# A fused two-model block on one core: the first stage put in written order, its state space products on VectorE alone with their matmuls by column groups, and its small loads on other queues

## The chip, the core and the metric

The kernel runs as one program on one core of a Trainium2 chip. The time is the device time of one execution in microseconds (us); the median of several runs is compared. Beside the times there is one profiled execution. In its rows PE is TensorE's matmuls, PEld its weight loads, DVE is VectorE, ACT ScalarE, POOL GpSimd; SPq and a DMA row of POOL are transfers being issued by SyncE and GpSimd.

## The reference

Two model blocks run one after the other on 256 tokens of width 1024, all in float32. The first has two attention layers (neighbourhood, then sliding window) with adaptive norms, whose shifts and scales come from a condition vector; the second has a grouped complex state space layer (S5) and a stick-breaking attention layer. What matters here is the start of the first block and the constants of the S5 layer, which the kernel works out early because they depend on weights alone:

```python
mod_lat = (silu_c @ ada_w[i] + ada_b[i])[:, None, :]      # 1024 x 6144 weights per layer
sh1, sc1, ga1, sh2, sc2, ga2 = jnp.split(mod_lat, 6, axis=-1)
u_lat = modulate(rms_norm(h_lat, g_mix[i]), sh1, sc1)     # 256 tokens; the same for 256 of context
ql, kl, vl = jnp.split((u_lat @ w).reshape(B, L, 3, H, dh), 3, axis=2)
...
a_bar = jnp.exp(lam * dt)                                 # 64 groups x 64 states, complex
b_bar = ((a_bar - 1.0) / lam)[..., None] * b_mat          # 64 x 64 x 16
bu = jnp.einsum('tbgh,gph->tbgp', u_t, b_bar)
a_cum, s = lax.associative_scan(binop, (a_elems, bu), axis=0)
y = jnp.einsum('tbgp,ghp->tbgh', s + a_cum * h0[None], c_mat).real
```

The kernel replaces the scan by chunks of 8 steps. For that it needs the powers of `a_bar` (0 to 8) times `b_bar`, called `em` or e below, their products with `c_mat` (a 128 x 128 kernel of each group pair, called k), and writes both to DRAM for the later S5 stage.

## The kernel before

A tile framework traces the program and a scheduler decides the order of the instructions on each engine; semaphores are added for every dependency. Each engine then runs its list strictly in order. Products in float32 are made of three passes: each weight is split into a high part (`whi`, by ScalarE) and a rest (`wlo`, by VectorE), the activations into `xh` and `xl`, and L299 to L301 are the three matmuls.

The first stage is L878 to L957. It holds these strands, which share the engines:

- The condition and S5 loads, the constants `cst`, and the tokens `x` and `ctx`, which TensorE transposes (L921) and ScalarE copies to `h` and `hc`.
- Sixteen ada steps (L342 to L374, `ada_step`): each loads 512 KB of `ada_w` and multiplies it by the condition in four column groups of TensorE (L357). Steps 0 to 7 make the shift, 8 to 15 the scale; after the 8th and the 16th step the sum is copied (`adacc`, L361), transposed (L364) and written to `mods`. Even steps load into three `ada` buffers, odd ones into pairs of halves `stl`, so about six steps can be in flight; a further load waits for the matmul of the step that held its buffer.
- S5's constants: `S5.__init__` makes the powers `pw` and `bb` on VectorE in small operations. `e(r, engine)` multiplies them for r = 0 to 3, each in 24 operations of 128 x 256: r = 0 and 1 on VectorE, r = 2 and 3 on GpSimd (L916, L917, L934, L940). `k1(r)` (L720, L723) multiplies e with the C matrix on TensorE into 32 columns of PSUM per group q, `et(r)` (L734) transposes e, ScalarE copies the result and SyncE writes it to `edr`; `k2(r)` (L742) transposes k.
- 22 small loads (L201, L903, L905), spread among the ada steps on SyncE.
- `rstd` (L425, L436): the sum of squares of the tokens; and `normed` (L463), which needs `mods`, makes `xh` and `xl` from the tokens, in eight steps for both streams.

The first attention stage begins with the query, key and value products of the first head pair (`g` and `sc` banks, L299 to L301), then score, softmax and the rest in chains, with the next pair's products between them (L971 to L1132). Two loops that set the order in the first stage:

```python
            s5.e(0, V)
            s5.e(2, G)
...
            for i in range(8):
                ada_step()
                some(3)
...
            for r in range(4):
                s5.k1(r)
                s5.et(r)
                s5.k2(r)
```

Of the kernel before, what the change touches and what calls it, by code (L numbers as in the profile page):

```python
# [16 lines left out]
D = 1024  # L17
# [65 lines left out]
def _build(ctx, tc, I, out, dbg):  # L83
# [3 lines left out]
    dma = nc.sync.dma_start  # L87
# [81 lines left out]
    def vector_loads(va, cc):  # L169

        def r128(ap):
            return ap.rearrange("(a b) -> a b", b=128)

        def r128l(ap):
            return ap.rearrange("l (a b) -> (l a) b", b=128)

        todo = [(cc[0:8, :], I["c"].rearrange("a (k p) -> (a k) p", p=128)),
                (cc[8:16, :], I["c_ctx"].rearrange("(k p) -> k p", p=128))]

        def rows(t, r0, src):  # L180
# [390 lines left out]
    def s5_load(pp):  # L571
# [15 lines left out]
        return (lt, ld, dr, bt, ci), [lambda o=o, i=i: dma(out=o, in_=i) for o, i in todo]  # L587

    class S5:


        def __init__(self, pp, loads):
# [55 lines left out]
            tb = [tmp_tile().rearrange("p (g h) -> p g h", h=16) for _ in range(2)]  # L648
            cmul(bb, bt, cb, tb)
# [7 lines left out]
            self.pf_, self.ph_ = pf, ph  # L657
            for r in range(2):
                act(pf[:, r], pw[r][:, 1:9, :], AF.Copy)
            u = [(cs, sn), (s_[7], s_[8])]  # L660
            for i in range(3):
                cmul((ph[:, 0], ph[:, 1]) if i == 2 else u[(i + 1) % 2], u[i % 2], u[i % 2], (t0, t1))

            self.em = [[pp.tile([128, 4, 2, 8, 16], F32, name=f"e{r}{i}") for i in range(2)] for r in range(3)]
            self.tm = [spare(2 + i, f"tm{i}").rearrange("p (i j t h) -> p i j t h", i=2, j=2, t=8) for i in range(2)]
            self.kt = [None] * 4
            self.ci, self.dr = ci, dr
# [27 lines left out]
        def save(self):  # L695
            for i in range(2):
                dma(out=cdr[:, 512 * i:512 * i + 512], in_=self.ct[i].rearrange("p g h -> p (g h)"))
            dma(out=cdr[:, 1024:1536], in_=self.pf_.rearrange("p r t g -> p (r t g)"))
            dma(out=cdr[:, 1536:1632], in_=self.ph_.rearrange("p i g -> p (i g)"))

        def e(self, r, eng):
            em, tm = self.em[r], [self.tm[eng is G][:, i] for i in range(2)]
            pa = [x_[:, 0:8, :].rearrange("p t (q j) -> p q j t", q=4)[:, :, 2 * r:2 * r + 2, :] for x_ in self.pw]
            ma = [x_.rearrange("p (q j) h -> p q j h", q=4)[:, :, 2 * r:2 * r + 2, :] for x_ in self.bb]
# [23 lines left out]
        def et(self, r):  # L728
            for q in range(4):
# [7 lines left out]
                dma(out=edr[:, 16 * q + 4 * r:16 * q + 4 * r + 4, :], in_=et)  # L737
# [128 lines left out]
    with ExitStack() as sa:  # L866
# [10 lines left out]
        pp = spp.enter_context(tc.tile_pool(name="pp", bufs=1))  # L877
        with ExitStack() as s0:  # L878
# [14 lines left out]
            for nm in ("x", "ctx"):  # L893
                for t in range(2):
                    r = [stage("h", len(xt) * 2 + j) for j in range(2)]
                    for j in range(2):
# [6 lines left out]
                lambda: dma(out=rp[:, :, 48:79],  # L903
                            in_=I["na_rpb"][0].rearrange("h r c -> (h r) c").rearrange("(p a) c -> p a c", a=2)),
                lambda: dma(out=rpad.rearrange("(p a) c -> p a c", a=2), in_=rp)]  # L905

            def some(n):
                for f in small_loads[0:n]:
                    f()
                del small_loads[0:n]  # L910

            for f in vloads[0:2] + [lambda: dma(out=cst, in_=I["cst"])] + sloads[0:5] + xloads:
                f()
            prep_cond(cc, sc)
            s5 = S5(pp, loads)
            s5.e(0, V)  # L916
            s5.e(2, G)  # L917
            for k in range(KT):
                ps = bank("x")
                for t in range(4):  # L920
                    T.transpose(ps[:, t * 128:(t + 1) * 128], xt[t][k // 4][:, (k % 4) * 128:(k % 4) * 128 + 128], ident)  # L921
                act(h[k], ps[:, 0:256], AF.Copy)
                act(hc[k], ps[:, 256:512], AF.Copy)
            for i in range(8):
                ada_step()
                some(3)
                ada_step()
                some(3)
                if i == 0:
                    for f in sloads[5:]:  # L930
                        f()
                if i == 1:
                    s5.c()
                    s5.e(3, G)  # L934
                if i == 2:
                    act(small, h[KT - 2][:, 0:1], AF.Sqrt, bias=eps, scale=0.0)
                    r = rstd(512, 0, None, "s")
                    prep_vectors(va)
                if i == 2:
                    s5.e(1, V)  # L940
            some(99)
            stt(gna, gna, 0.125, swg[:, 208:272], MUL, MUL)
            ts(gsw[0], gsw[0], 0.125, MUL)
            w = I["na_wqkv"][0]
            w_first = [Weights(wpairs(w, D, 0), by_k=True),
                       Weights(wcols(w, 2 * D, 256), by_k=True)]
            x = new_x(xa, "x", 512)
            normed(x, r, 512, lambda k, v: scg[0][:, 0, k, v:v + 1], lambda k, v: modcol(0, 0, k, v))
            for r in range(4):
                s5.k1(r)  # L950
                s5.et(r)
                s5.k2(r)
            s5.zero()
# [876 lines left out]
```

## Time and profile before

| | before |
|---|---|
| median of 3 runs | 1811.14 us (1809.02 to 1816.51) |
| the profiled execution: its time | 1810.93 us |
| its span, first to last instruction | 1809.2 us |
| busy share of the span | PE 95%, PEld 83%, DVE 66%, ACT 44%, POOL 26% |
| mean granted TensorE clock | 0.978 of full speed |

A busy share says how much of the span an engine had an instruction in work. TensorE is busy nearly throughout; its idle time is found by stretches, and the first stretch is where this change lies.

### The profile page before, as it was taken

The page shows a single profiled execution, that of the slowest core. Times are in us where ns is not written, and L with a number is a line of the kernel's source. Part 1 is how long each engine was busy: PE and PEld are TensorE (multiplying, and loading weights), DVE is VectorE, ACT ScalarE, POOL GpSimd, SP SyncE. Part 2 cuts the span into 40 slices and gives each one's busy share as a digit, 9 for nine tenths or more (in the row PEclk, how much of TensorE's full clock was granted, in tenths as well). Part 3 has the DMA queues.
Part 4 walks back from the last instruction along what each step waited for, and adds up shares of the span by engine and source line. Part 5 has one row for each costly group of instructions (what it writes and reads, how often), then busy time and mean ns, then how long its engine had stood idle before and what let it go on. Part 6 is the DMA issues. An engine that isn't in the chain of part 4 may idle for free. (4 is left out here: it accounts for less than half of the span.)

```text
span 1809.2 us, 33749 instructions
## 1 busy us (share of the span) xinstructions
PE 1717.4 (95%) x13129; PEld 1504.4 (83%) x13129; DVE 1197.0 (66%) x2508; ACT 790.6 (44%) x1446; POOL 470.6 (26%) x633
## 2 busy tenths in 40 slices
PE   5799999989999999999978999989999999999999
PEld 3478888867777777888757999978899999789998
DVE  8556877865545334447987656768577788958674
ACT  4343444433313132324655545536444465544443
POOL 5312211225789000040002000211331322424130
PEclk8899999999999999999989999999999999999999
DMA  8565555434676554332107566698458564336852
GB/s 219 174 174 160 148 169 154 109 96 134 205 220 202 180 180 141 93 97 74 53 24 186 153 196 183 208 308 225 128 154 233 150 211 142 115 97 167 231 154 88
DMA packets 441042, 286.56 MB, mean 158 GB/s; under 512 B 50450, under 2 KB 418610, under 8 KB 440882
## 3 DMA queue, kind: packets, MB, share of 16 engines
q1 hardware_dynamic: 439122, 278.64, 53.3%
q0 software_dynamic: 1760, 5.77, 0.8%
q8 instruction: 103, 1.69, 0.4%
q14 instruction: 57, 0.47, 0.1%
HBM read 271.41 MB, written 17.15 MB: 159 GB/s over the span
## 5 line engine op out<-in xcount | busy, mean ns | idle before, releaser
L108 ACT ACTIVATE whi<-raw 128x1024 fp32r<-128x1024 f32 (+2 forms) x388 | 389.7, 1012 | 487.8 <-PE g L292 353.1
L111 DVE TENSOR_TENSOR wlo<-raw,whi 128x1024 fp32r<-128x1024 f32 (+2 forms) x388 | 469.1, 1214 | 185.7 <-ACT whi L108 182.9
L293 PE MATMUL g<-xh,wlo 128*128 128x256 f32 (+1 forms) x1216 | 375.3, 309 | 5.6 <-DVE wlo L111 5.2
L291 PE MATMUL g<-xh,whi 128*128 128x256 f32 (+1 forms) x1216 | 375.5, 310 | 1.3 <-ACT xh L108 1.2
L292 PE MATMUL g<-xl,whi 128*128 128x256 f32 (+1 forms) x1216 | 374.7, 308 | 0.0
L291 PE MATMUL g<-oh,whi 128*128 128x256 f32 (+1 forms) x1056 | 332.1, 315 | 3.9 <-DVE hc L114 1.4
L293 PE MATMUL g<-oh,wlo 128*128 128x256 f32 (+1 forms) x1056 | 331.5, 314 | 0.0
L292 PE MATMUL g<-ol,whi 128*128 128x256 f32 (+1 forms) x1056 | 331.1, 314 | 0.0
L293 PEld LDWEIGHTS g<-xh,wlo 128*128 128x128 f32 x1216 | 235.4, 194 | 18.0 <-DVE wlo L111 7.4
L291 PEld LDWEIGHTS g<-xh,whi 128*128 128x128 f32 x1216 | 234.9, 193 | 16.4 <-ACT whi L108 3.5
L292 PEld LDWEIGHTS g<-xl,whi 128*128 128x128 f32 x1216 | 235.7, 194 | 9.6
L291 PEld LDWEIGHTS g<-oh,whi 128*128 128x128 f32 x1056 | 198.1, 188 | 25.1 <-issue 3.9
L292 PEld LDWEIGHTS g<-ol,whi 128*128 128x128 f32 x1056 | 198.4, 188 | 15.1 <-issue 0.9
L293 PEld LDWEIGHTS g<-oh,wlo 128*128 128x128 f32 x1056 | 198.4, 188 | 14.5 <-issue 0.3
L299 PE MATMUL g<-whi,xh 128*128 128x256 f32 x560 | 167.5, 299 | 3.8 <-ACT xh L108 2.8
L300 PE MATMUL g<-wlo,xh 128*128 128x256 f32 x560 | 161.6, 289 | 0.6 <-DVE wlo L111 0.6
L301 PE MATMUL g<-whi,xl 128*128 128x256 f32 x560 | 160.3, 288 | 0.1
L114 DVE SCALAR_TENSOR_TENSOR h<-g,mods,h 128x256 f32<-128x256 f32 x64 | 30.8, 483 | 139.1 <-PE g L293 139.1
L299 PEld LDWEIGHTS g<-whi,xh 128*128 128x128 f32 x560 | 108.3, 193 | 14.6 <-issue 10.0
L300 PEld LDWEIGHTS g<-wlo,xh 128*128 128x128 f32 x560 | 108.6, 194 | 2.0 <-DVE wlo L111 1.6
L301 PEld LDWEIGHTS g<-whi,xl 128*128 128x128 f32 x560 | 108.0, 194 | 1.1 <-issue 0.4
L108 ACT ACTIVATE oh<-t 128x256 fp32r<-128x256 f32 (+1 forms) x108 | 51.3, 482 | 125.5 <-DVE t L111 125.5
(300 smaller groups left out, 2892.0 us busy)
## 6 DMA issues: line engine op xcount, KB each, us to landing
raw<-mlp_w SPq DMA_DIRECT2D x128, 512.0 KB, 4.3
ada<-ada_w SPq DMA_DIRECT2D x88, 512.0 KB, 6.4
raw<-ffn_w_up SPq DMA_DIRECT2D x88, 512.0 KB, 5.4
raw<-ffn_w_down SPq DMA_DIRECT2D x32, 384.0 KB, 3.9
raw<-ffn_w_down SPq DMA_DIRECT2D x32, 320.0 KB
raw<-na_wqkv SPq DMA_DIRECT2D x32, 256.0 KB, 4.1
raw<-a_w_glu SPq DMA_DIRECT2D x16, 512.0 KB, 7.5
raw<-w_kv SPq DMA_DIRECT2D x16, 512.0 KB, 4.3
```

Source lines behind the costliest of these rows:

```text
L108: last[0] = A.activation(out=o, in_=i, func=f, **kw)
L111: (e or V).tensor_tensor(out=o, in0=a, in1=b, op=op)
L114: V.scalar_tensor_tensor(out=o, in0=a, scalar=s, in1=b, op0=op0, op1=op1)
L291: T.matmul(ps, lhsT=a, rhs=xh[k][:, s0:s1], start=first, stop=False)
L292: T.matmul(ps, lhsT=a, rhs=xl[k][:, s0:s1], start=False, stop=False)
L293: T.matmul(ps, lhsT=b, rhs=xh[k][:, s0:s1], start=False, stop=last_)
L299: T.matmul(ps, lhsT=xh[k][:, t0:t0 + 128], rhs=a, start=first, stop=False)
L300: T.matmul(ps, lhsT=xh[k][:, t0:t0 + 128], rhs=b, start=False, stop=False)
L301: T.matmul(ps, lhsT=xl[k][:, t0:t0 + 128], rhs=a, start=False, stop=last_)
```

## The change

Everything in the first stage up to the second weight load of the first head pair is traced inside a region in which all five engines keep the order in which the code is written. In that order the ada steps are dealt out by hand: 4, 2, 3, 2, 2 and 3 steps, with the S5 pieces between. All four `e(r)` run on VectorE, in 12 operations of 128 x 512 each, on operands that are laid out again: GpSimd copies the powers to `pw2` (eight small operations) and `bb` is written in the order that e reads. In `k1` the four column groups q are now the innermost loop. The S5 loads and the writes of `edr` and `cdr` are issued by ScalarE, the small loads by GpSimd. The pool `pp` is taken from the other end of the memory.

```diff
-    dma = nc.sync.dma_start
+    dma, dma_a = nc.sync.dma_start, nc.scalar.dma_start
...
-        return [lambda o=o, i=i: dma(out=o, in_=i) for o, i in todo]
+        return [lambda o=o, i=i, n=n: (dma if n < 2 else G.dma_start)(out=o, in_=i) for n, (o, i) in enumerate(todo)]
...
-        return (lt, ld, dr, bt, ci), [lambda o=o, i=i: dma(out=o, in_=i) for o, i in todo]
+        return (lt, ld, dr, bt, ci), [lambda o=o, i=i: dma_a(out=o, in_=i) for o, i in todo]
...
+        def tables(self):
+            pp, pw, pf, ph, u = self.pp, self.pw, self.pf_, self.ph_, self.u
+            self.pw2 = [pp.tile([128, 32, 8], F32, name=f"pz{i}") for i in range(2)]
+            for i in range(2):
+                for r in range(4):
+                    ts(self.pw2[i][:, 8 * r:8 * r + 8, :].rearrange("p (q j) t -> p q j t", q=4),
+                       pw[i][:, 0:8, :].rearrange("p t (q r j) -> p r q j t", q=4, r=4)[:, r], 1.0, MUL, 0.0, ADD, e=G)
...
-        def e(self, r, eng):
-            em, tm = self.em[r], [self.tm[eng is G][:, i] for i in range(2)]
...
-            for q in range(4):
-                cmul([x_[:, q] for x_ in em], [x_[:, q].unsqueeze(3).to_broadcast([128, 2, 8, 16]) for x_ in pa],
-                     [x_[:, q].unsqueeze(2).to_broadcast([128, 2, 8, 16]) for x_ in ma], tm, e=eng)
+        def e(self, r):
+            for hf in range(2):
+                g = slice(8 * r + 4 * hf, 8 * r + 4 * hf + 4)
+                cmul([x_.rearrange("p q j t h -> p (q j) t h")[:, 4 * hf:4 * hf + 4] for x_ in self.em[r]],
+                     [x_[:, g, :].unsqueeze(3).to_broadcast([128, 4, 8, 16]) for x_ in self.pw2],
+                     [x_[:, g, :].unsqueeze(2).to_broadcast([128, 4, 8, 16]) for x_ in self.bb], self.tm)
...
-            for q in range(4):
-                for jp in range(2):
-                    for i in range(2):
+            for jp in range(2):
+                for i in range(2):
+                    for q in range(4):
                         T.matmul(kp[32 * q:32 * q + 32, jp * 128:(jp + 1) * 128],
                                  lhsT=cbk[i][:, q, jp].rearrange("p j h -> p (j h)"),
                                  rhs=em[i][:, q, jp].rearrange("p t h -> p (t h)"), start=i == 0, stop=False)
+                for q in range(4):
                     T.matmul(kp[32 * q:32 * q + 32, jp * 128:jp * 128 + 16], lhsT=self.dd[:, 8 * q + 2 * r + jp, :],
                              rhs=C("dm")[0:32, :], start=False, stop=True)
...
-                dma(out=edr[:, 16 * q + 4 * r:16 * q + 4 * r + 4, :], in_=et)
+                dma_a(out=edr[:, 16 * q + 4 * r:16 * q + 4 * r + 4, :], in_=et)
...
-        pp = spp.enter_context(tc.tile_pool(name="pp", bufs=1))
+        pp = spp.enter_context(tc.tile_pool(name="pp", bufs=1, side="right"))
...
+            with tc.manual_schedule(engines={ENG.PE, ENG.DVE, ENG.Activation, ENG.SP, ENG.Pool}):
+                for f in vloads[0:2] + [lambda: dma(out=cst, in_=I["cst"])] + sloads + xloads + small_loads[0:15]:
+                    f()
+                prep_cond(cc, sc)
+                s5 = S5(pp, loads)
...
+                s5.tables()
+                for f in small_loads[15:]:
+                    f()
+                ada(4)
+                s5.c()
+                s5.e(0)
+                ada(2)
+                act(small, h[KT - 2][:, 0:1], AF.Sqrt, bias=eps, scale=0.0)
+                r_ = rstd(512, 0, None, "s")
+                prep_vectors(va)
+                ada(3)
+                s5.e(1)
+                operators(0)
+                ada(2)
+                w_first = [Weights(wpairs(w, D, 0), by_k=True)]
+                ada(2)
+                s5.e(2)
...
+                operators(1)
+                ada(3)
+            w_first.append(Weights(wcols(w, 2 * D, 256), by_k=True))
+            x = new_x(xa, "x", 512)
+            normed(x, r_, 512, lambda k, v: scg[0][:, 0, k, v:v + 1], lambda k, v: modcol(0, 0, k, v))
+            operators(2)
+            s5.e(3)
+            operators(3)
```

The orders below are those of the two built programs; the attention stage and what follows keep theirs but for a few hundred rows at its beginning. First VectorE, where the S5 products begin (`tm` is a partial product, `e` a result, `pw` or `pz` the powers, `bb` the B matrix, `ph` a later phase, `dd` a diagonal from the loaded `dr`). Before:

```order
L111 TENSOR_TENSOR ph<-sm 128x32
L111 TENSOR_TENSOR tm_273<-pw_198,bb_219 128x256
L111 TENSOR_TENSOR pw_199<-t 128x128
L111 TENSOR_TENSOR sm<-sm 128x32 x2
L111 TENSOR_TENSOR tm_273<-pw_199,bb_220 128x256
L111 TENSOR_TENSOR ph<-sm 128x32
L111 TENSOR_TENSOR e_267<-tm_273 128x256
```

VectorE in the same place after the change:

```order
L112 TENSOR_TENSOR pw_221<-t 128x128
L112 TENSOR_TENSOR sm<-sm 128x32 x14
L112 TENSOR_TENSOR ph<-sm 128x32
L112 TENSOR_TENSOR sm<-sm 128x32 x2
L112 TENSOR_TENSOR ph<-sm 128x32
L112 TENSOR_TENSOR dd<-dr,cst 32x1024
L112 TENSOR_TENSOR tm_361<-pz_325,bb_241 128x512
L112 TENSOR_TENSOR tm_362<-pz_326,bb_242 128x512
L112 TENSOR_TENSOR e_355<-tm_361,tm_362 128x512
```

The first e operation no longer mixes with the powers: it stands behind `dd`, and `dd` behind all of the phases. Second, TensorE at the first k1, before (`e_267` and `e_268` are the two parts of e(0), L357 is an ada step, L212 and L734 transposes):

```order
L357 MATMUL x<-ada,sl 32x256 x4
L720 MATMUL s<-e_267,cbk 32x128
L720 MATMUL s<-e_268,cbk 32x128
L734 MATMUL s<-cst,e_267 128x128 x2
L723 MATMUL s<-cst,dd 32x16
L720 MATMUL s<-e_267,cbk 32x128
L720 MATMUL s<-e_268,cbk 32x128
L212 MATMUL x<-cst,va 128x128
L723 MATMUL s<-cst,dd 32x16
```

TensorE at the first k1 after the change:

```order
L437 MATMUL s<-sd,cst 128x128 x4
L213 MATMUL x<-cst,va 128x128 x3
L358 MATMUL x<-ada,sl 32x256 x4
L358 MATMUL x<-stl_544,sl 32x256 x2
L358 MATMUL x<-stl_545,sl 32x256 x2
L365 MATMUL x<-cst,adacc 128x128 x2
L358 MATMUL x<-ada,sl 32x256 x4
L734 MATMUL s<-e_355,cbk 32x128 x4
L734 MATMUL s<-e_356,cbk 32x128 x4
L738 MATMUL s<-cst,dd 32x16 x4
```

Nine ada steps now stand before the first k1 instead of three, and four matmuls of four column groups follow each other where there were two of one group. Third, VectorE where `normed` begins, before:

```order
L111 TENSOR_TENSOR e_270<-tm_273 128x256
L114 SCALAR_TENSOR_TENSOR swg<-swg 128x64
L124 COPY adacc<-x 128x256
L111 TENSOR_TENSOR mods_71<-x,vt 128x4x2 x2
L124 COPY adacc<-x 128x256
L111 TENSOR_TENSOR mods_71<-x,vt 128x4x2 x2
L114 SCALAR_TENSOR_TENSOR scg_73<-mods_71,vt 128x16
L114 SCALAR_TENSOR_TENSOR t<-h_77,scg_73,s 128x256
```

VectorE where `normed` begins after the change:

```order
L112 TENSOR_TENSOR e_360<-tm_361,tm_362 128x512
L115 SCALAR_TENSOR_TENSOR swg<-swg 128x64
L120 TENSOR_SCALAR swg<-swg 128x64
L125 COPY adacc<-x 128x256
L112 TENSOR_TENSOR tm_361<-pz_325,bb_241 128x512
L112 TENSOR_TENSOR mods_71<-x,vt 128x4x2 x2
L112 TENSOR_TENSOR tm_362<-pz_326,bb_242 128x512
L115 SCALAR_TENSOR_TENSOR scg_73<-mods_71,vt 128x16
L112 TENSOR_TENSOR e_436<-tm_361,tm_362 128x512
L115 SCALAR_TENSOR_TENSOR t<-h_77,scg_73,s 128x256
```

The second `adacc` copy now stands behind e(0), e(1) and e(2) with the four weight splits between them, 36 operations of 128 x 512, and three of e(3)'s operations lie between it and `normed`; the other nine of e(3) stand behind `normed`.

## Rows read from the trace of the kernel before

**Rows 1.** The page: the span

```profile
span 1809.2 us, 33749 instructions
```

**Rows 2.** Windows: busy time of each engine by stretch, granted clock, DMA share

```profile
0.00:30.00 30.00, 14.62 (x102) 10.09 (x103) 21.50 (x86) 16.53 (x45) 10.08 (x21) 0.94 0.92 225
30.00:60.00 30.00, 23.77 (x183) 14.65 (x181) 28.39 (x38) 9.51 (x27) 28.04 (x38) 0.88 0.46 149
60.00:79.70 19.70, 12.48 (x105) 4.39 (x101) 5.07 (x17) 3.25 (x8) 0.41 (x1) 0.83 0.64 203
79.70:127.70 48.00, 46.74 (x366) 40.23 (x367) 26.85 (x81) 24.24 (x59) 3.88 (x6) 0.96 0.61 177
...
140.00:390.00 250.00, 247.01 (x2116) 207.38 (x2114) 193.87 (x616) 117.28 (x301) 46.70 (x55) 0.99 0.47 138
```

**Rows 3.** Timeline, 74 to 80: start, length, what, idle before

```profile
74.36 1.05 PE L357 MATMUL x<-ada,sl 128*32 128x256 f32 x8 [2.34 <-DMA ada<-ada_w]
...
77.01 0.42 DVE L124 COPY adacc<-x 128x256 f32<-128x256 f32 x1 [8.20 <-PE x L357]
...
79.68 0.79 PE L299 MATMUL g<-whi,xh 128*128 128x256 f32 x2 [1.59 <-ACT xh L108]
```

**Rows 4.** Groups on VectorE to 79.7 and on GpSimd; timeline, 20 to 22

```profile
L111 DVE TENSOR_TENSOR tm<-pw,bb 128x256 f32<-128x256 f32 x32 | 24.3, 795 | 0.5
...
L111 DVE TENSOR_TENSOR t<-bt,sm 128x512 f32<-128x512 f32 x4 | 2.7, 683 | 0.0
...
L111 POOL TENSOR_TENSOR tm<-pw,bb 128x256 f32<-128x256 f32 x32 | 24.5, 782 | 20.0 <-DVE pw L111 18.8
...
20.94 0.41 DVE L111 TENSOR_TENSOR tm<-pw,bb 128x256 f32<-128x256 f32 x1
```

**Rows 5.** TensorE: groups from 79.7 to 127.7; timeline at 89

```profile
L720 PE MATMUL s<-e,cbk 128*32 128x128 f32 x64 | 10.1, 278 | 0.3 <-ACT et L108 0.2
...
L734 PE MATMUL s<-cst,e 128*128 128x128 f32 x40 | 6.7, 306 | 0.0
...
L357 PE MATMUL x<-ada,sl 128*32 128x256 f32 x8 | 0.6, 391 | 0.0
...
89.18 0.62 PE L720 MATMUL s<-e,cbk 128*32 128x128 f32 x4
...
89.90 0.62 PE L720 MATMUL s<-e,cbk 128*32 128x128 f32 x4
```

**Rows 6.** Issues: SyncE's timeline at 4, 21 and 83; GpSimd's group

```profile
3.88 3.23 SPq L587 DMA_DIRECT2D bt<-a_b_im  x1
...
20.92 1.74 SPq L587 DMA_DIRECT2D ci<-a_c_im  x2
...
83.00 2.95 SPq L737 DMA_DIRECT2D edr<-et  x4
...
L812 POOL DMA_DIRECT2D fdr<-fm x16 | 11.5, 716 | 4.8 <-POOL fm L121 4.8
```

**Rows 7.** Timeline of VectorE; groups of TensorE to 79.7

```profile
8.71 0.29 DVE L124 COPY L<-s 128x128 f32<-128x128 f32 x1 [0.41 <-PE s L604]
...
21.27 0.28 DVE L111 TENSOR_TENSOR pw<-t 128x128 f32<-128x128 f32 x1
...
L676 PE MATMUL s<-cst,ci 128*128 128x128 f32 x16 | 2.8, 336 | 0.0
...
L436 PE MATMUL s<-sd,cst 128*128 128x128 f32 x8 | 2.0, 437 | 4.0 <-DVE sd L429 4.0
```

**Rows 8.** Groups on VectorE, 78 to 127.7

```profile
L114 DVE SCALAR_TENSOR_TENSOR xl<-t,mods,xh 128x256 fp32r<-128x256 f32 x16 | 7.2, 481 | 8.1 <-ACT xh L108 8.0
...
L111 DVE TENSOR_TENSOR wlo<-raw,whi 128x1024 fp32r<-128x1024 f32 x4 | 4.9, 1221 | 3.4 <-ACT whi L108 3.4
```

**Rows 9.** Windows after the first scores; timeline of their first product

```profile
128.00:132.00 4.00, 1.86 (x16) 1.03 (x16) 1.30 (x4) 2.88 (x6) 0.00 (x0) 1.00 0.81 246
...
127.71 0.28 PE L1079 MATMUL sc<-a,q 128*128 128x256 f32 x1
```

More of the change, by code (lines that the diff above doesn't have):

```diff
@@ L86, in _build @@
     MUL, ADD, SUB = ALU.mult, ALU.add, ALU.subtract
-    dma = nc.sync.dma_start
+    dma, dma_a = nc.sync.dma_start, nc.scalar.dma_start
+    ENG = mybir.EngineType
     const = ctx.enter_context(tc.tile_pool(name="const", bufs=1))
@@ L647, in __init__ @@
             cb = [c_.unsqueeze(2).to_broadcast([128, 32, 16]) for c_ in (c0, c1)]
-            tb = [tmp_tile().rearrange("p (g h) -> p g h", h=16) for _ in range(2)]
-            cmul(bb, bt, cb, tb)
+            tb = [tmp_tile() for _ in range(2)]
+            t_ = [x_.rearrange("p (g h) -> p g h", h=16) for x_ in tb]
+            tv = [x_.rearrange("p (q r n) -> p q r n", q=4, r=4) for x_ in tb]
+            bv = [x_.rearrange("p (r q j) h -> p q r (j h)", r=4, q=4) for x_ in bb]
+            for i in range(2):
+                tt(t_[0], bt[0], cb[i], MUL)
+                tt(t_[1], bt[1], cb[1 - i], MUL)
+                tt(bv[i], tv[0], tv[1], ADD if i else SUB)
             k = 1
@@ L657, in __init__ @@
             self.pf_, self.ph_ = pf, ph
+            self.ci, self.dr = ci, dr
+            self.u, self.t_ = [(cs, sn), (s_[7], s_[8])], (t0, t1)
+        def tables(self):
[5 more added lines that the diff above has]
+                       pw[i][:, 0:8, :].rearrange("p t (q r j) -> p r q j t", q=4, r=4)[:, r], 1.0, MUL, 0.0, ADD, e=G)
             for r in range(2):
                 act(pf[:, r], pw[r][:, 1:9, :], AF.Copy)
-            u = [(cs, sn), (s_[7], s_[8])]
             for i in range(3):
-                cmul((ph[:, 0], ph[:, 1]) if i == 2 else u[(i + 1) % 2], u[i % 2], u[i % 2], (t0, t1))
+                cmul((ph[:, 0], ph[:, 1]) if i == 2 else u[(i + 1) % 2], u[i % 2], u[i % 2], self.t_)
             self.em = [[pp.tile([128, 4, 2, 8, 16], F32, name=f"e{r}{i}") for i in range(2)] for r in range(3)]
-            self.tm = [spare(2 + i, f"tm{i}").rearrange("p (i j t h) -> p i j t h", i=2, j=2, t=8) for i in range(2)]
+            self.tm = [spare(2 + i, f"tm{i}").rearrange("p (n t h) -> p n t h", n=4, t=8) for i in range(2)]
             self.kt = [None] * 4
-            self.ci, self.dr = ci, dr
         def c(self):
@@ L696, in save @@
             for i in range(2):
-                dma(out=cdr[:, 512 * i:512 * i + 512], in_=self.ct[i].rearrange("p g h -> p (g h)"))
-            dma(out=cdr[:, 1024:1536], in_=self.pf_.rearrange("p r t g -> p (r t g)"))
-            dma(out=cdr[:, 1536:1632], in_=self.ph_.rearrange("p i g -> p (i g)"))
-        def e(self, r, eng):
-            em, tm = self.em[r], [self.tm[eng is G][:, i] for i in range(2)]
-            pa = [x_[:, 0:8, :].rearrange("p t (q j) -> p q j t", q=4)[:, :, 2 * r:2 * r + 2, :] for x_ in self.pw]
-            ma = [x_.rearrange("p (q j) h -> p q j h", q=4)[:, :, 2 * r:2 * r + 2, :] for x_ in self.bb]
-            for q in range(4):
-                cmul([x_[:, q] for x_ in em], [x_[:, q].unsqueeze(3).to_broadcast([128, 2, 8, 16]) for x_ in pa],
-                     [x_[:, q].unsqueeze(2).to_broadcast([128, 2, 8, 16]) for x_ in ma], tm, e=eng)
+                dma_a(out=cdr[:, 512 * i:512 * i + 512], in_=self.ct[i].rearrange("p g h -> p (g h)"))
+            dma_a(out=cdr[:, 1024:1536], in_=self.pf_.rearrange("p r t g -> p (r t g)"))
+            dma_a(out=cdr[:, 1536:1632], in_=self.ph_.rearrange("p i g -> p (i g)"))
+        def e(self, r):
[4 more added lines that the diff above has]
+                     [x_[:, g, :].unsqueeze(2).to_broadcast([128, 4, 8, 16]) for x_ in self.bb], self.tm)
         def k1(self, r):
@@ L716, in k1 @@
             kp = bank("s")
-            for q in range(4):
-                for jp in range(2):
-                    for i in range(2):
+            for jp in range(2):
+                for i in range(2):
+                    for q in range(4):
                         T.matmul(kp[32 * q:32 * q + 32, jp * 128:(jp + 1) * 128],
@@ L902, in _build @@
             small_loads = vloads[2:] + [
[L903 to L949, printed above, removed]
+                lambda: G.dma_start(out=rp[:, :, 48:79],
+                                    in_=I["na_rpb"][0].rearrange("h r c -> (h r) c").rearrange("(p a) c -> p a c", a=2)),
@@ L950, in _build, with ada, operators @@
+                lambda: G.dma_start(out=rpad.rearrange("(p a) c -> p a c", a=2), in_=rp)]
+            def ada(n):
+                for _ in range(n):
+                    ada_step()
+            def operators(r):
                 s5.k1(r)
@@ L952, in _build @@
                 s5.k2(r)
+            w = I["na_wqkv"][0]
+            with tc.manual_schedule(engines={ENG.PE, ENG.DVE, ENG.Activation, ENG.SP, ENG.Pool}):
[3 more added lines that the diff above has]
+                s5 = S5(pp, loads)
+                for k in range(KT):
+                    ps = bank("x")
+                    for t in range(4):
+                        T.transpose(ps[:, t * 128:(t + 1) * 128], xt[t][k // 4][:, (k % 4) * 128:(k % 4) * 128 + 128],
+                                    ident)
+                    act(h[k], ps[:, 0:256], AF.Copy)
+                    act(hc[k], ps[:, 256:512], AF.Copy)
+                s5.tables()
[15 more added lines that the diff above has]
+                s5.e(2)
+                stt(gna, gna, 0.125, swg[:, 208:272], MUL, MUL)
+                ts(gsw[0], gsw[0], 0.125, MUL)
+                operators(1)
[6 more added lines that the diff above has]
+            operators(3)
             s5.zero()
```

## The prediction

> **What bounds the kernel now.** I read the span first, then a table of windows, to see where TensorE is not the bound. The span is 1809.2 us [rows 1], the execution's own time 1810.93. From 140 to 390 us TensorE works 247 of 250 us [rows 2]: there the program runs at TensorE's pace, and whatever makes that stage begin earlier comes out of the total one for one. Before 79.7 us it is different: TensorE is busy 14.6, 23.8 and 12.5 us in the first three windows [rows 2], much of it in small matmuls. What the first attention products wait for is the scale vector: the last ada step's load arrives at 74.36, its sum is copied at 77.01 after VectorE stood idle for 8.2 us, and the first product (L299) starts at 79.68 [rows 3]. The DMA share falls from 0.92 to 0.46 and is 0.64 in the third window [rows 2], so bandwidth isn't what delays that load. Loads are held because TensorE's list has an ada step behind k1 products that wait for e; the step's buffer comes free late. From 79.7 to 127.7 TensorE is the bound, 46.7 of 48 us [rows 2], but 10.1 us are k1 products and 6.7 us transposes of e [rows 5]. The first scores start at 127.71, and in the next 4 us TensorE works only 1.9 [rows 9].
>
> So two things count: **when the first product starts** (79.7 now), and **how much S5 work is left on TensorE behind it**.
>
> **The first product after the change.** I follow VectorE's new list, since it holds everything in one row.
>
> It first reaches `dd`, which needs the last S5 load transposed by TensorE, and in TensorE's list that stands behind four ada steps. By then the constants (0.70 MB), the tokens (2.10), the B and C matrices (0.52 and 1.05) and four ada steps (2.10) must have landed, 6.47 MB; the first window moved 225 GB/s [rows 2], so that is 28.7 us. One ada step takes 0.6 us (eight entries, [rows 5]), the 16 transposes L676 2.8 [rows 7], the last copy and `dr` about 1.0, `dd`, as wide as two operations of 512, 1.4. VectorE starts e(0) at 34.5. What comes before has room. The chain of powers ran from 8.71 to 21.55 [rows 7]; ScalarE must now issue ten loads before its first activation. On SyncE one such issue took 3.23 us and two took 1.74 [rows 6]: at most 3.2 + 9 x 0.87 = 11.1 us. Even if the powers move by 9 us for it, they end by 30.6; the eight copies on GpSimd, priced at its 0.78 us for 256 columns [rows 4] though they are 64 wide, end by 36.9 at worst, 2.4 us later than 34.5; with short issues (0.45 us each) they are done long before. I take 34.5.
>
> The price of an e operation decides next. Beside GpSimd an operation of 128 x 256 took VectorE 0.795 us, and GpSimd's own 0.782; the one at 20.94, when GpSimd was between two operations, took 0.41, and operations of 128 x 512 of the same kind took 0.683 [rows 4]. GpSimd has no e work any more, so 0.683 it is: 8.2 us for each e(r). The lower bound is the same row less its start-up, about 0.60; the upper is twice 0.795. On the Trainium skill's page "SBUF — State Buffer", section "SBUF: two separate sides", VectorE operations with two SBUF inputs and GpSimd operations that read SBUF exclude each other on a shared port; the 0.41 against 0.795 agrees with it.
>
> From 34.5: e(0) to 42.7. Then VectorE's reciprocal goes to TensorE (four products, 2.0 us, [rows 7]), two ada steps (1.2), `adacc` (0.4) and some five steps of 0.4 between engines, 5.6 together: this loop is a **new stall**, since VectorE's next row needs the end of it. At 48.3 e(1), to 56.5; four weight splits at 1.22 us [rows 8] and e(2), 13.1, to 69.6; `adacc`, three e(3) operations and the small ones, 3.4, to 73.0; one operation on each of VectorE and ScalarE, and the first product starts at **74.0**, 5.7 us earlier. The ada loads have to be in by about 60 for this: the last four can be issued when steps 6 to 8 are through TensorE at 47, and 2.1 MB at 225 GB/s need 9.3 us, to 56.
>
> **TensorE behind it.** k1 now takes 0.72 us for each pair of products in one column group (89.18 to 89.90, [rows 5]), 5.7 us for a k1(r), and two of the four stand behind the first product: 11.5 us. After the change one is left, k1(3), with its four column groups in turn. The ada steps show what that is worth: four products of 256 columns in four groups took 0.6 us [rows 5], so four of 128 take 0.3, and k1(3) with its six sets 1.8. That gives 9.7. The bounds are 0 for this part (a product waits for the one that it adds to, as now) and 10.3. Of the 40 transposes of e in the window 16 remain; 24 at 0.17 us [rows 5] are 4.0. Together 13.7.
>
> Behind 127.7 the 2.1 idle us [rows 9] go too: the new list puts the next pair's products ahead of the first scores. Against this I set 1 us of new waiting. VectorE's list puts nine e(3) operations and two weight splits (8.6 us) between `normed` and the head statistics. `normed` is 16 operations `xl` (7.2 us, [rows 8]) and 16 `t` of about the same length, so from 73.0 it ends at 87.8 and the rest at 96.4. TensorE's 192 products take some 23.5 of the 48 us (the window less its other work), so with k1(3) and the transposes it is fed until 102, and then by the next pair: nearly covered.
>
> **Edits at nothing.** The small loads leave SyncE, whose issues aren't on the path above. GpSimd issues a load in 0.716 us [rows 6]; 15 end at 12, before the powers. The 16 `edr` writes cost ScalarE what they cost SyncE, 0.74 us each (four in 2.95, [rows 6]), 12 us; ScalarE is busy 24.2 of 48 us in the last window [rows 2], so they delay `xh` by one issue at times. If that cover is gone, it's up to 3 us. The pool's other end changes no wait that the rows show.
>
> **Sum.** 5.7 + 13.7 + 2.1 - 1.0 = 20.5; 1810.9 - 20.5 = **1790**; the median of the three runs lies 0.2 above the profiled time.
>
> **Rivals.**
> 1. The written order gains no time ahead of the first product: one landing or one issue comes 6 us late, and VectorE's list passes it on whole. For it speaks that `dd`, the reciprocal and both `adacc` copies each wait for TensorE; against it, that the ada loads have some 4 us of room. The gain is then 14.8: 1796.
> 2. GpSimd's loads are starved. It must issue 15 of them before the copies of the powers. If it can issue none while VectorE runs operations with two inputs, about half of them would wait for the powers' end at some 27, then 5 us of issues and 6 of copies: e(0) at 38 to 39, and 1794. If each issue took 2.5 us, three and a half times the row, it would be e(0) at 45: 1801. The same page's warning "DVE blocks DMA" says such loads starve under VectorE's two-port operations. By its 3.1 us an issue e(0) would start near 54, and the sum would be 1809, no gain. Against it, the row's 16 issues show no wait of that size in their mean of 0.716 us [rows 6].
> 3. Slower: VectorE's price isn't contention but the operand pattern, with the 0.41 an exception. At 1.59 us (twice 0.795) 36 operations cost 32.8 us more before the first product and nine 8.2 behind `normed`, of which TensorE's products cover most: 1790 + 33 = 1823. It decides from 1.25 us an operation on (20.5 / 36 = 0.57 over 0.683). Against it: 0.41 and 0.683, both measured on broadcast operands.
> 4. The column groups don't overlap in k1: 9.7 less, 1800.
>
> **How the numbers follow.** The forecast 0.55 (1784 to 1797), rival 1 0.15, rival 2 0.10 (a third of it with no gain), rival 3 0.05, rival 4 0.07; 0.08 for a better case, e(0) at 28 because the loads land sooner: 1784 and below. The range 1779 to 1803 leaves out rival 3, the worst of rival 2 and some mishaps. 0.5% is 9 us, about what a measurement of this kernel can tell: faster 0.85, same 0.10, slower 0.05.
>
> **What would show it.** VectorE's e operations near 0.68 us and e(0) near 34.5; a wait of VectorE for TensorE ahead of `dd`; the first L300 product at 74; k1 in under 2 us; TensorE dense from there on. An e operation over 1.2 us, a first product after 85, or GpSimd still issuing loads at 30 would prove me wrong.

## The result, and the profile after

The changed kernel takes 1801.16 us (median, 1795.42 to 1804.82), the kernel before 1813.89 in the same comparison: a ratio of 0.9933, 95% interval 0.9918 to 0.9947, some 12 us. The forecast was 1790. The sign held, and the time lies in the stated range (1779 to 1803), though outside the band that I had given the forecast itself (1784 to 1797). Of the 20.5 us of gain about 60% came, all of it behind the first product.

The profiled execution took 1804.82 us (span 1803.1), the slowest of its six; so I compare landmarks inside the trace. The first attention product moved from 79.68 [rows 3] to 85.66: 6.0 us **later**, where I forecast 5.7 earlier. The first scores moved from 127.71 [rows 9] to 119.50, the last ones of the first attention layer from 388.2 to 378.1. So 16.1 us were won behind the first product and 6.0 lost ahead of it: 10.1. Behind the last scores, which the change leaves alone, this trace took 4.0 us more than the one before (1425.0 and 1421.0); over the traces of all runs that part varies from 1418.8 to 1427.3. The first product after the change, then the score products before and after (all of them, with first and last start):

```profile
85.66 0.39 PE L300 MATMUL g<-whi,xh 128*128 128x256 f32 x1
...
L1079 PE MATMUL sc<-a,q x96: 276/283/562, 127.7 to 388.2; 128*128 128x256 f32 x96
...
L1097 PE MATMUL sc<-a,q x96: 276/283/583, 119.5 to 378.1; 128*128 128x256 f32 x96
```

Windows of the kernel after, to be held against [rows 2] (window and length, then busy time of PE, PEld, DVE, ACT, POOL, granted clock, DMA share, GB/s):

```profile
0.00:30.00 30.00, 6.19 (x30) 5.97 (x31) 4.90 (x28) 6.99 (x17) 8.80 (x24) 1.00 0.97 248
80.00:85.60 5.60, 5.38 (x51) 3.43 (x51) 4.30 (x13) 3.24 (x9) 0.00 (x0) 0.70 0.60 194
85.60:91.60 6.00, 5.94 (x49) 5.61 (x50) 5.96 (x16) 4.27 (x12) 0.00 (x0) 1.00 0.24 91
119.50:131.80 12.30, 12.30 (x105) 12.00 (x104) 7.43 (x29) 5.04 (x15) 2.95 (x5) 1.00 0.74 185
```

In the first 30 us VectorE works 4.9 us, where it worked 21.5: something holds it. ScalarE's timeline of the kernel after says what (ACTq rows are transfers that ScalarE issues):

```profile
2.67 7.04 ACTq L588 DMA_DIRECT2D bt<-a_b_im  x1
9.75 5.05 ACTq L588 DMA_DIRECT2D ci<-a_c_re  x2
14.84 2.88 ACTq L588 DMA_DIRECT2D ci<-a_c_im  x2
20.48 0.33 ACTq L588 DMA_DIRECT2D dr<-a_d  x1
20.85 1.28 ACT L109 ACT_TABLE_LOAD   x1 [20.85 <-DMA ci<-a_c_im]
```

Its ten issues last until 20.8 us, and its first activation waits behind them. VectorE and TensorE need what its first activations make (`sc`, `ld`), so everything slides. VectorE's timeline, in the order of my steps (`L`, end of the powers, `dd`, e(0), the loop's reciprocal, e(1), the second `adacc`, `normed`):

```profile
24.88 0.29 DVE L125 COPY L<-s 128x128 f32<-128x128 f32 x1 [0.40 <-PE s L605]
38.49 0.29 DVE L112 TENSOR_TENSOR pw<-t 128x128 f32<-128x128 f32 x1
42.49 1.21 DVE L112 TENSOR_TENSOR dd<-dr,cst 32x1024 f32<-32x1024 f32 x1 [0.40 <-ACT dr L109]
43.64 1.27 DVE L112 TENSOR_TENSOR tm<-pz,bb 128x512 f32<-128x512 f32 x2
44.95 0.69 DVE L112 TENSOR_TENSOR e<-tm,tm 128x512 f32<-128x512 f32 x1
51.72 0.94 DVE L430 RECIPROCAL sd<-sd 128x128 f32<-128x128 f32 x1
57.75 1.28 DVE L112 TENSOR_TENSOR tm<-pz,bb 128x512 f32<-128x512 f32 x2
80.15 0.42 DVE L125 COPY adacc<-x 128x256 f32<-128x256 f32 x1
83.27 0.47 DVE L115 SCALAR_TENSOR_TENSOR t<-h,scg,s 128x256 f32<-128x256 f32 x1
```

`L` came at 8.71 before [rows 7], so it is 16.2 us later; at e(0) 9.1 us of lateness against my 34.5 are left, and nothing behind it gives them back.

TensorE's groups of the kernel after, from the first product to the first scores (85.6 to 119.5), against [rows 5]:

```profile
L749 PE MATMUL s<-cst,e 128*128 128x128 f32 x16 | 2.7, 279 | 0.0
L734 PE MATMUL s<-e,cbk 128*32 128x128 f32 x32 | 1.9, 282 | 0.0
L738 PE MATMUL s<-cst,dd 32*32 32x16 f32 x16 | 0.5, 188 | 0.0
```

One k1 is left there, with its four column groups at once, and 16 transposes. (A product of k1 stands as two matmul rows in the trace: the 16 of k1(3) are the x32.)

### The profile page after: what moved, and what is told of

It reads as the page before. It is cut to its first block, busy times and chain, and to the rows that moved or that the text cites. A ratio compares the mean times of both kernels' runs of the same rounds, so it can differ in the third digit from the quotient of the medians.

```text
span 1803.1 us, 33711 instructions
## 1 busy us (share of the span) xinstructions
PE 1694.5 (94%) x13129; PEld 1492.9 (83%) x13129; DVE 1195.4 (66%) x2508; ACT 792.1 (44%) x1446; POOL 446.9 (25%) x615
```

## The experiments

Each was timed in five rounds against the kernel before; the ratio is to that kernel, so the experiments can be compared with each other through it. A difference of 0.001 is 1.8 us.

**1. The S5 loads back on SyncE (s5_loads_on_sp).**

```diff
-        return (lt, ld, dr, bt, ci), [lambda o=o, i=i: dma_a(out=o, in_=i) for o, i in todo]
+        return (lt, ld, dr, bt, ci), [lambda o=o, i=i: dma(out=o, in_=i) for o, i in todo]
```

> The changed kernel, with the ten loads of the S5 weights issued by SyncE at the same place of the list (behind the constants, ahead of the tokens). Theory A, ScalarE's list is held by its own issues (7.04, 5.05 and 2.88 us, first activation at 20.85): the first activation comes at about 3, the powers end by 24, and e(0) starts where the last S5 load and four ada steps let it, at 36 to 38 instead of 43.6; the first attention product moves from 85.7 to about 79.5, and the time falls by 5 to 7 us to 1794 to 1796. Theory B, the loads themselves land late and the issue only waits with them: first activation early, but e(0) not before 42, and the time stays at 1800 to 1802.

Measured: 1791.05 us, 0.9889 (0.9875 to 0.9902), 8 us below the change, more than theory A asked; it beats both kernels. SyncE's issues, VectorE's `dd`, and TensorE's first product in this run:

```profile
3.88 3.86 SPq L588 DMA_DIRECT2D bt<-a_b_im  x1
7.78 3.01 SPq L588 DMA_DIRECT2D ci<-a_c_re  x2
10.83 1.93 SPq L588 DMA_DIRECT2D ci<-a_c_im  x2
13.76 1.85 SPq L912 DMA_DIRECT2D sth<-x  x4
...
32.67 1.21 DVE L112 TENSOR_TENSOR dd<-dr,cst 32x1024 f32<-32x1024 f32 x1 [6.87 <-ACT dr L109]
...
75.74 0.58 PE L300 MATMUL g<-whi,xh 128*128 128x256 f32 x1
```

e(0) starts at 33.8 (forecast 34.5), the first product at 75.7 (74.0), and the time is 1791 (1790): with this one line undone my sum holds, 3.9 us of it ahead of the first product (5.7 forecast) and 17.0 from there to the last scores at 367.3 (14.8 forecast). On SyncE's list the ten issues run from 2.02 to 13.71, 11.7 us against the 11.1 that I had reckoned; on ScalarE's they ended at 20.8. The longest, `bt<-a_b_im`, took 7.04 us there and 7.36 and 7.46 in the two other runs with these loads on ScalarE, and 3.23 to 4.01 in the eleven with them on SyncE. The tokens' issues in the kernel after are longer than here as well:

```profile
2.42 4.32 SPq L912 DMA_DIRECT2D sth<-x  x4
13.18 4.27 SPq L912 DMA_DIRECT2D sth<-ctx  x4
```

But that does not come from the second list alone: in the kernel before and in experiment 12, with all these loads on SyncE and the tokens right behind `bt<-a_b_im`, the first four took 3.73 and 4.09 us too.

**2. In that kernel, e(0) ahead of the ada steps and of `dd` (s5_loads_on_sp_e0_first).**

```diff
+                s5.e(0)
                 ada(4)
                 s5.c()
-                s5.e(0)
                 ada(2)
```

> As the kernel with the S5 loads on SyncE, and e(0) written ahead of the four ada steps and of the transposes of the C matrix with the diagonal dd. If dd is what holds e(0), as I forecast, e(0) starts when the powers and GpSimd's eight copies are done, at 26 to 30, and the next row to wait for is the reciprocal, which needs the sums of squares behind ScalarE's copies of C: about 44 to 46, so e(1) at 50 to 52, the first product at 77 to 78, and 1792 to 1794. Rival: e(0) was not on the path at all, the ada loads are; then nothing more than with the S5 loads on SyncE alone.

Measured: 1791.88 us, 0.9890 (0.9873 to 0.9907), no difference: the rival's time, with the theory's wait. e(0) now follows the phases at 25.7 and ends 8 us sooner, but the wait only moves on, to the row that I had named:

```profile
40.14 0.95 DVE L430 RECIPROCAL sd<-sd 128x128 f32<-128x128 f32 x1 [5.17 <-ACT sd L109]
```

Without e(0)'s lateness the reciprocal comes at 40.14 instead of 41.90; `normed` and the first product (73.8) start 2 us earlier, which is within the interval.

**3 and 4. The loops of k1: exchanged in the kernel before (before_k1_by_groups), put back in the kernel after (after_k1_old_loops).**

```diff
-            for q in range(4):
-                for jp in range(2):
-                    for i in range(2):
+            for jp in range(2):
+                for i in range(2):
+                    for q in range(4):
...
+                for q in range(4):
```

> The kernel before, with the loops of k1 exchanged alone (the four column groups innermost). My term: k1(2) and k1(3) stand behind the first product, 16 sets at 0.72 us become 3.6 us instead of 11.5; the first product stays at 79.7 within 1 us, and the time falls by 7 to 9 us to 1805 to 1807. Rival, column groups do not overlap because a product waits for the one it adds to: within 1 us of before, 1813 to 1815.

> The changed kernel, with the loops of k1 as before (column groups outermost). If the loop order gave what I forecast, k1(3) costs 3.9 us more behind the first product, and k1(0) to k1(2), now in front of it on an idle TensorE, between 0 and 4 us more: 1804 to 1809. Rival, no overlap of column groups: 1800 to 1802.

Measured: before with the new loops 1801.72 us, 0.9948 (0.9936 to 0.9960); after with the old loops 1816.51 us, 1.0031 (1.0019 to 1.0043), slower than before. So the exchange is worth 9.4 us in the old order and 17.7 in the new one ((1.0031 - 0.9933) x 1811). In the first run, behind the first product (79.19, unmoved), the 64 matmul rows of [rows 5] that took 10.1 us:

```profile
L720 PE MATMUL s<-e,cbk 128*32 128x128 f32 x64 | 2.9, 289 | 0.2 <-ACT et L108 0.2
```

In the second, k1(1), the transposes of the second `adacc`, which came at 81.13 in the kernel after, and the window from 73 to 80:

```profile
74.23 1.06 PE L734 MATMUL s<-e,cbk 128*32 128x128 f32 x4
...
75.44 1.06 PE L734 MATMUL s<-e,cbk 128*32 128x128 f32 x4
...
92.67 0.38 PE L365 MATMUL x<-cst,adacc 128*128 128x128 f32 x2
...
73.00:80.00 7.00, 7.00 (x37) 4.13 (x36) 4.30 (x7) 0.21 (x1) 0.00 (x0) 0.52 0.37 118
```

I had taken the k1 ahead of the first product as free, since TensorE is idle there. In the written order they stand ahead of the ada steps in TensorE's list, so their length delays the scale vector: 11.5 us. Part of it is the clock: in the window 73 to 80 TensorE is busy throughout at a granted clock of 0.52, near the lower of its two levels (1.2 GHz). There a pair of products takes 1.2 us, where it takes 0.72 at 1.00 [rows 5]; for the six pairs from 73.14 to 80.23 that is 2.8 us, by estimate (7.1 - 6 x 0.72).

**5. The S5 loads on SyncE, without the written order (s5_sp_scheduler_order).**

```diff
-            with tc.manual_schedule(engines={ENG.PE, ENG.DVE, ENG.Activation, ENG.SP, ENG.Pool}):
+            with ExitStack():
```

> The kernel with the S5 loads on SyncE, without the region that keeps the written order: the scheduler decides the order of the same instructions. If the written order is worth what its steps gave in that kernel (first product at 75.7 instead of 79 or later, 24 transposes ahead of it), this run is slower than 1791 by 5 to 12 us: 1796 to 1803, with a first product behind 79. Rival, the written order gains nothing and the gain is k1's loops, e on VectorE and the queues: 1789 to 1793.

Measured: 1793.96 us, 0.9890 (0.9878 to 0.9903), the ratio of experiment 1 (0.9889): the rival. The scheduler's order has its first product at 73.80, earlier than the written one.

**6. The same line in the changed kernel, S5 loads on ScalarE (after_scheduler_order).**

> The changed kernel, S5 loads on ScalarE as it has them, without the region that keeps the written order. With the S5 loads on SyncE the written order was worth 1.5 us at most. If ScalarE's held list costs the same 8 to 10 us in either order: 1799 to 1804. Rival, the written order passes the lateness on and the scheduler's order, in which e(0) does not stand behind dd and four ada steps, absorbs it: 1792 to 1797.

Measured: 1801.10 us, 0.9945 (0.9931 to 0.9959), against 0.9933 with the written order. ScalarE issues until 26.3 there, and the lateness costs 10 us (0.9945 - 0.9890), against 8 in the written order. The written order as such gains nothing that can be measured, in either setting. This run also shows that the start of the first product alone is no measure of the time. Here it is 17 us earlier than in the kernel after:

```profile
68.52 0.56 PE L300 MATMUL g<-whi,xh 128*128 128x256 f32 x1
```

The first scores come at 119.3, against 119.5: 92 k1 rows and 43 transposes stand behind that product instead of 32 and 16, and TensorE is idle for 3.9 us until the scores instead of 1.0.

**7. In the kernel of experiment 1, the writes of `edr` and `cdr` on SyncE (s5_sp_edr_on_sp).**

```diff
-                dma_a(out=edr[:, 16 * q + 4 * r:16 * q + 4 * r + 4, :], in_=et)
+                dma(out=edr[:, 16 * q + 4 * r:16 * q + 4 * r + 4, :], in_=et)
```

(and the three writes of `cdr`)

> The kernel with the S5 loads on SyncE, with the writes of edr and cdr issued by SyncE too, as before the change. My term: these writes cost ScalarE nothing that shows; then 1789 to 1793, at best 3 us less. Rival: in the written order SyncE must wait for each et before it issues what stands behind, the later ada and weight loads among it; then the second adacc copy moves from 69.7 to 73 or later and the time is 1794 to 1800.

Measured: 1812.22 us, 0.9994 (0.9985 to 1.0004): 19 us lost, more than twice the rival's highest price. SyncE's list, then TensorE and VectorE, in this run:

```profile
52.31 2.24 SPq L752 DMA_DIRECT2D edr<-et  x4
54.60 0.94 SPq L353 DMA_DIRECT2D stl<-ada_w  x2
...
57.51 1.77 PE L358 MATMUL x<-stl,sl 128*32 128x256 f32 x8 [3.39 <-DMA stl<-ada_w]
...
86.67 0.43 DVE L125 COPY adacc<-x 128x256 f32<-128x256 f32 x1 [2.86 <-PE x L358]
```

From 35.2 to 52.3 SyncE issues nothing, because its next row waits for `et`; the ada loads behind it start late, and the second `adacc` moves from 69.66 to 86.67.

**8. In the kernel of experiment 1, the small loads on SyncE (s5_sp_small_loads_on_sp).**

```diff
-        return [lambda o=o, i=i, n=n: (dma if n < 2 else G.dma_start)(out=o, in_=i) for n, (o, i) in enumerate(todo)]
+        return [lambda o=o, i=i, n=n: dma(out=o, in_=i) for n, (o, i) in enumerate(todo)]
```

(and the loads of `rp` and `rpad`)

> The kernel with the S5 loads on SyncE, with the small loads issued by SyncE too, at their place in the list (15 behind the tokens, seven behind the phases). Theory: GpSimd's queue keeps some 8 us of issues (15 at 0.4 to 0.6) out of SyncE's way; the first ada loads go out at 24 to 26 instead of 17.6, e(0) starts at 38 to 41 instead of 33.9, and the time is 1795 to 1798. Rival: SyncE has room and the DMA engines are the limit: 1790 to 1792.

Measured: 1806.43 us, 0.9963 (0.9950 to 0.9976), 13 us lost; the theory, with a size that was too small. I had counted 15 issues; all 22 stand ahead of the ada loads, and the last waits for the one before it to land. SyncE and TensorE:

```profile
34.47 0.36 SPq L920 DMA_DIRECT2D rpad<-rp  x1
34.88 0.38 SPq L353 DMA_DIRECT2D ada<-ada_w  x1
...
38.89 1.08 PE L358 MATMUL x<-ada,sl 128*32 128x256 f32 x8 [12.48 <-DMA ada<-ada_w]
```

**9. The kernel before, with k1 by groups and both kinds of transfer moved (before_k1_queues).** Edits as in 3, 7 and 8, in the kernel before, the last two the other way round.

> The kernel before, with k1 by column groups (0.9948), and besides with the writes of edr and cdr on ScalarE and the 22 small loads on GpSimd; the S5 loads stay on SyncE, e stays divided between VectorE and GpSimd, and the scheduler decides the order. Theory: most of what the changed kernel with S5 loads on SyncE has over this one's basis (0.9890 against 0.9948, some 10 us) is the emptied list of SyncE, as moving these transfers back cost 21 and 15 us there: 1791 to 1796. Rival: it is e on VectorE alone, free of the shared pace with GpSimd; then 1800 to 1803, or more where GpSimd's loads stand in front of its e.

Measured: 1803.45 us, 0.9958 (0.9944 to 0.9971), no better than the loops alone (0.9948). My theory falls: in the scheduler's order the emptied list gains nothing. The two moves were tried together only, so a gain by one and a loss by the other are not excluded. The e operations of VectorE still run beside GpSimd's (0.806 and 0.687 us for 256 columns).

**10. The kernel of experiment 5, with e(2) and e(3) back on GpSimd (s5_sp_sched_e23_gpsimd).**

```diff
+        def e(self, r, eng=None):
+            n = 2 if eng is G else 4
+            tm = [self.tg[:, i] for i in range(2)] if eng is G else self.tm
...
                 s5.e(0)
+                s5.e(2, G)
+                s5.e(3, G)
```

(and the two calls of e(2) and e(3) further down left out)

> The run in the scheduler's order with the S5 loads on SyncE (0.9890), with e(2) and e(3) given back to GpSimd, in 24 operations of 128 x 256 each as before the change; e(0) and e(1) stay on VectorE in 12 operations of 128 x 512. Theory: the 10 us that lie between this basis and the kernel before with k1 and the queues changed (0.9958) are e on VectorE alone; then e operations cost 0.75 us and more on both engines again, TensorE waits for e, and the time is 1800 to 1806. Rival: they come from the order in which the code is traced and from the pool's place; then 1792 to 1797.

Measured: 1801.38 us, 0.9930 (0.9918 to 0.9943): e on VectorE alone is worth 7 us (0.9930 - 0.9890). Groups of GpSimd and VectorE in this run, 20 to 80, and last VectorE's in experiment 5, alone:

```profile
L112 POOL TENSOR_TENSOR tg<-pz,bb 128x256 f32<-128x256 f32 x32 | 27.6, 879 | 1.2
...
L112 DVE TENSOR_TENSOR tm<-pz,bb 128x512 f32<-128x512 f32 x16 | 14.5, 938 | 0.9 <-POOL pz L122 0.8
```

```profile
L112 DVE TENSOR_TENSOR tm<-pz,bb 128x512 f32<-128x512 f32 x28 | 18.3, 687 | 0.5 <-POOL pz L122 0.2
```

The same operation takes 0.94 us beside GpSimd and 0.69 without.

**11 and 12. Two further orders on the basis of experiment 1 (reordered, reordered_tokens_first).** The diff is the second's, which also loads the tokens ahead of C; the first has four and two ada steps around the sums of squares, and e(2) behind `normed`:

```diff
-                ada(4)
-                s5.c()
                 s5.e(0)
                 ada(2)
...
                 r_ = rstd(512, 0, None, "s")
+                ada(4)
+                s5.c()
...
-                operators(0)
                 ada(2)
                 w_first = [Weights(wpairs(w, D, 0), by_k=True)]
+                operators(0)
```

> A version that goes on from the S5 loads on SyncE: e(0) ahead of the ada steps, the sums of squares ahead of the C matrix's transposes (the run with e(0) first waited 5.2 us there for ScalarE's squares), the first head pair's weights ahead of operators(0), e(2) written behind normed. If VectorE's list sets the first product, the reciprocal starts at 36 to 37 instead of 40 to 42, e(1) at 42 to 44, and the first product at 65 to 69 instead of 75.7: with some 1.5 us of transposes moved behind it, 1782 to 1787. Rival: the ada loads, 14.9 MB with all others at 225 to 250 GB/s, set it: first product at 70 to 73, 1788 to 1791.

> A second version that goes on from the S5 loads on SyncE: the C matrix and dr are loaded behind the tokens, e(0) and the sums of squares stand ahead of the C matrix's transposes, the first weights ahead of operators(0), and e(2) stays ahead of normed so that no work moves behind the first product. If VectorE's list sets the pace: tokens transposed by 22, reciprocal at 31 to 34, first adacc at 38 to 40, first product at 66 to 69, 1782 to 1786. Rival: TensorE's steps and the ada buffers set it, each load waits for the step that held its buffer: first product at 73 to 76 and no gain, 1789 to 1793.

Measured: 1793.03 us, 0.9882 (0.9867 to 0.9897), and 1793.41 us, 0.9902 (0.9890 to 0.9915): neither differs from experiment 1. The first has its first product at 71.29, 4.4 us earlier, but first scores at 108.7 against 109.8 and last ones at 368.0 against 367.3. The window up to the scores holds 24 transposes, 52 rows of k1 and 32 of `dd`, 8.0 us against 5.1: 2.9 us of the gain are given back as TensorE's work, the rest in small waits. In the second I made a wait of my own, with `dd` ahead of `adacc` in VectorE's list and ScalarE's C copies behind the squares:

```profile
44.91 1.21 DVE L112 TENSOR_TENSOR dd<-dr,cst 32x1024 f32<-32x1024 f32 x1 [10.29 <-ACT dr L109]
```

Its first product comes at 75.88, so it doesn't test whether loads or VectorE's list would set the pace without that wait.

## Why the prediction was right, and where it was wrong

**The step that failed** is "ScalarE must now issue ten loads before its first activation ... at most 3.2 + 9 x 0.87 = 11.1 us". They lasted until 20.8 us. I had carried over issue times of a list in which SyncE sent one transfer after the other; here two lists sent at once, and one issue took 7.04 us, two 5.05. With it fell "Even if the powers move by 9 us for it, they end by 30.6": they end at 38.8, past the room that I had counted up to 34.5. Experiment 1 shows both: without ScalarE's issues, e(0), the first product and the time come within 2 us of the forecast.

By the prediction's own sign, "a first product after 85", the part ahead of the first product was wrong: it came at 85.66, 11.7 us after the forecast's 74.0. GpSimd also still issued loads at 30, another of its signs, but those are the seven that stand behind the copies of the powers, and they came late with the powers. That the time still fell into the range is luck: the range reached to 1803 for other mishaps, and a part that went wrong by 11.7 us left the time 2 us inside it.

The Trainium skill's page "DMA: Bandwidth & Descriptors", section "Issuing engines are not separate DMA queues", says that transfers of all issuers share the same 16 DMA engines and that several issuers save only issue time. The first windows agree with sharing: 248 GB/s with two lists, 259 in experiment 1 with one. That such an issue is usually small against its transfer does not hold for ScalarE here: the issue of `bt<-a_b_im` took 7.04 us, and its 256 KB landed 12.5 us from the issue.

**Rows that held.** The e operations: 0.65 and 0.69 us against 0.683, so rival 3 falls. The loop from the reciprocal to e(1): 6.0 us against 5.6. GpSimd's 15 loads, 0.50 to 0.71 us each, end at 12.45 against 12; so rival 2 falls, though VectorE had not begun by then. Column groups overlap, so rival 4 falls.

Experiment 2 has GpSimd's later loads beside VectorE's two-input operations on SBUF, which is what rival 2 was about:

```profile
26.21 0.53 POOL L202 DMA_DIRECT2D swg<-na_k_gain  x1
26.73 0.80 POOL L918 DMA_DIRECT2D rp<-na_rpb  x1
36.76 0.55 POOL L920 DMA_DIRECT2D rpad<-rp  x1 [9.23 <-DMA rp<-na_rpb]
...
25.67 1.29 DVE L112 TENSOR_TENSOR tm<-pz,bb 128x512 f32<-128x512 f32 x2
```

The issues take 0.53 and 0.80 us, as in experiment 1, where VectorE is idle from 25.8 to 32.7. The warning "DVE blocks DMA" of the Trainium skill's page "SBUF — State Buffer" (section "SBUF: two separate sides") does not show in them. It is a warning of two-port operations such as a float32 copy, and the 3.1 us that I took from that page for an issue are there the time of a whole transfer beside such a copy. The load of `rp` lands 9.2 us after its issue, but VectorE's work is hardly what delays it: in experiment 1, with VectorE idle for most of that time, it took 8.3:

```profile
35.92 0.55 POOL L920 DMA_DIRECT2D rpad<-rp  x1 [8.33 <-DMA rp<-na_rpb]
```

The shared port of which the same section of the Trainium skill tells agrees with experiment 10 (0.94 us beside GpSimd, 0.69 without).

**TensorE behind the first product** was forecast at 13.7 + 2.1 - 1.0 = 14.8 and measured 16.1. k1 went from 11.5 to 2.4 us (9.1 against 9.7: four products in four groups took 0.43 us, not 0.3), the transposes from 6.7 to 2.7 (4.0 as forecast). The 2.1 idle us right behind the first scores were filled: TensorE works 12.3 of 12.3 us there after, and 10.05 before. But more idle time came later, so that over the whole stretch from the first product to the last scores it grew from 6.0 to 8.3 us (the sums of windows): on balance this term gave nothing. In its place came the clock, which I had not counted: in the 6 us behind the first product it was granted 0.72 before and 1.00 after, in the 12.3 us behind the first scores 0.86 and 1.00 (1.00 is the upper of its two levels, 2.4 GHz), together some 3.4 us by estimate (6 x 0.28 + 12.3 x 0.14). These add up to 14.2 (9.1 + 4.0 - 2.3 + 3.4); the other 1.9 us I can't assign. In the kernel after the first product follows k1 and transposes with hardly a gap (the window 80 to 85.6: 5.38 busy, clock 0.70), where it followed 1.59 idle us [rows 3] before; no run changes this alone. The two windows of the kernel before are:

```profile
79.70:85.70 6.00, 5.27 (x25) 4.62 (x26) 4.80 (x9) 4.04 (x9) 0.00 (x0) 0.72 0.59 162
127.70:140.00 12.30, 10.05 (x66) 7.37 (x64) 6.89 (x10) 5.39 (x9) 4.10 (x4) 0.86 0.73 212
```

**"Edits at nothing"** was right beside the old order (experiment 9, both moves together), and wrong as a statement on the new one: there they cover 19 and 13 us (experiments 7 and 8).

**Rival 1** said that the written order gains nothing ahead of the first product, because one landing or one issue comes 6 us late and VectorE's list passes it on whole. That is what happened, at about twice the size: issues made e(0) 9.1 us late, the list passed it on, and the first product came 11.7 us after the forecast. Experiments 5 and 6 show more: no gain at all from the written order. The gain of the change is then made of k1's loops (9.4 us alone), e on VectorE (7 us), less 8 to 10 for the S5 loads on ScalarE. These were measured on different bases and need not add; what makes up the rest between experiment 10 (0.9930) and 9 (0.9958), some 5 us, stays open: the wider e operations on VectorE, the order of tracing and the pool's other end are all in it.

## What to carry to other kernels

An issue of a transfer can hold its engine for microseconds, so an engine whose first result others wait for should not issue large loads ahead of it. (ScalarE's ten here went out in small pieces: its queue moved 1.61 MB in 12576 packets in the first 30 us. Whether larger pieces would have held it less was not tried.) Price issues by rows in which as many lists send at once as will after the change. In a written order a list that waits holds what stands behind it, so what is off the path in a scheduler's order (k1 ahead of the first product, the writes of `et`) can be on it there; test each such edit in the order in which it will run.

## What the runs showed of the hardware

Moving the same ten loads from SyncE to ScalarE, while SyncE also sends, lengthened the longest of their issues (3.86 us in experiment 1, 7.04 in the kernel after) and moved no more data in the first 30 us (259 and 248 GB/s). Four k1 products in four column groups took 0.43 us (the row below, from the kernel after), two in one group 0.62 [rows 5], both at a granted clock of 1.00; the exchange of three loop lines is worth 9.4 to 17.7 us of a kernel of 1811.

```profile
68.62 0.43 PE L734 MATMUL s<-e,cbk 128*32 128x128 f32 x8 [2.09 <-ACT cbk L109]
```
